# Packing sample tokens by heads, 576 projected columns, a moved sum, and S5 powers written in part as copies

## The chip, the cores and the metric

The kernel runs on one core of a Trainium2 chip. The metric is device time in microseconds (us), the median of several runs. The engines are PE (TensorE, matrix products), DVE (VectorE), ACT (ScalarE), POOL (GpSimd) and SP (SyncE, which here only issues DMAs). Each executes its own list of instructions in order, and semaphores join them.

## What is computed

Two layers of a decoder trunk for 512 prompt tokens and 8 x 8 sample tokens, 576 in all, of width 1024. Layer 0 mixes tokens with S5, a complex diagonal state space; layer 1 with causal pooling. Each mixer is followed by a layer norm and by PEER, a mixture of 16384 single-row experts:

```python
q = (x @ w_q).reshape(T, 8, 2, 128)                # 8 heads, 2 halves
s = einsum('thid,hind->thin', q, keys)              # 128 keys per half
top_s, top_i = top_k(s, 16)
cand = top_s[:, :, 0, :, None] + top_s[:, :, 1, None, :]
best_s, best_j = top_k(cand.reshape(T, 8, 256), 16)
idx  = ...                                          # key a * 128 + key b
gate = softmax(best_s)
out  = sum over h, k of  gate * gelu(x . u[idx]) * v[idx]
```

In S5 each of 64 groups has 64 complex states; u = x @ w_in is turned into inputs of the states, these run through a recurrence in time, and y is read out with the matrices C times powers of the transition.

## The kernel before

**Tokens.** The kernel carries 640 columns (NX): 384 (ND) of tiles 0 to 2, then 128 of tile 3, and 128 of tile 4 in which the 64 sample tokens stand twice. NT is 576, the tokens without the second copy. Tiles 0 to 2 go through all experts densely, tiles 3 and 4 through gathered rows.

**S5** (`s5()`). `params()` makes the powers `PW` 0 to 8. For each of eight blocks m of features, `uproj` multiplies on PE and `udone` writes u to DRAM (`du`); after m=3 and m=7 it is read back as `U8` in 16 DMAs in all, rearranged by time step. From m=4 on, `back(q)` (DVE, two `BL` tiles per call, four in rotation) multiplies b by powers 7 to 0, and `turn(q)` transposes the tiles on PE. `taps(q)` (DVE) writes c times the powers 0 to 8 into `CL`. `inputs` (PE, ACT) needs U8 and the turned tiles, `toeplitz` the taps; then the recurrence `steps` runs on DVE.

**The score loop** (`peer()`, c = 0 to 15, one half of a head each). In each iteration PE projects (`projected`: 8 blocks x 3 split products, each over two column ranges 0 to ND and ND to NX), ACT and POOL prepare the next weight (`W.ahead`: for w_q the low half `wl`, L79, is subtracted on POOL), PE multiplies the previous q with its keys (`scores`, five tiles), and DVE takes the 16 largest of each tile (`tops`, L1347 to L1355) of the one before that. Ahead of the loop POOL adds xH and xL into `xT` (L1049), in the place of tiles 0 to 2 of x, which go to DRAM first.

**The routing** (`routing`, `stage2`) is a generator that is pulled beside this: up to PA=6 steps per iteration, and an iteration stops at a step STEP. Its first two units (g = 0, 1) take four heads' halves each of all five tiles, so n8 = 10 rows of heads; a later unit takes tiles 3 and 4 with the remaining four heads, n8 = 8, the next two tiles 0 to 2. Behind the loop a second loop with hand-set credits multiplies x with experts (44 blocks per layer), gathers rows and pulls the rest of the routing. Of tile 4, rows 0 to 63 then use the entries of heads 0 to 3, rows 64 to 127 those of heads 4 to 7, so that each copy of the samples does half of them; the halves are added at the end.

**Order around it.** `norms` ends the mixer: tile by tile, layer norm on DVE, transposes on PE; the products of groups 0 and 1 over columns 0 to ND are put in early (`early`), their remainders come first in the loop. L799 is a DVE operation on one column in that norm. `finish` does the same at the end of layer 0, and the pooling mixer too calls `projected`.

Of the kernel before, what the change touches and what calls it, by code (L numbers as in the profile page):

```python
# [19 lines left out]
KD = 8  # L20
SEQ = 512
NB = 8
TS = 64
NT = SEQ + TS
NC = 72
ND = 384
NX = 640
# [12 lines left out]
BT, GB, HC, PW = 1, 32, 2.0, (1,)  # L40
GE, S3, S4 = 0.98, 100, 4
VL = (43, 44, 45)
ORDER = [a for a in range(128) if (a + 1) * NPO // 128 > a * NPO // 128]
ORDER += [a for a in range(128) if a not in ORDER]
OFF = [0, 16, 24, 29, 33, 36, 38, 40] + list(range(42, 50))
# [81 lines left out]
class K:  # L127
# [142 lines left out]
    def s5(self):  # L270
# [55 lines left out]
        def powered(jobs, a, b):  # L326

            def args(e, w):
                n, k = e.stop - e.start, len(range(9)[w])
                sh = [128, n, k, 16]  # L330
                pw = [PW[:, w, r, e].rearrange("p s e -> p e s")[:, :, :, None].to_broadcast(sh) for r in range(2)]
                return pw, [t[:, e, None, :].to_broadcast(sh) for t in (a, b)]
            todo = [(o, t) + args(e, w) for o, t, e, w in jobs]
            for o, t, pw, ab in todo:
                V.tensor_tensor(o, pw[0], ab[0], op=OP.mult)
            for o, t, pw, ab in todo:
                V.tensor_tensor(t, pw[1], ab[1], op=OP.mult)
            for o, t, pw, ab in todo:
                V.tensor_tensor(o, o, t, op=OP.subtract)

        def params():
# [14 lines left out]
                next(ex, None)  # L356
            for _ in ex:
                pass
            V.memset(PW[:, 0, 0, :], 1.0)
            V.memset(PW[:, 0, 1, :], 0.0)  # L360
            V.tensor_tensor(PW[:, 1, 0, :], mag, cs, op=OP.mult)
            V.tensor_tensor(PW[:, 1, 1, :], mag, sn, op=OP.mult)
            tmp = p2.tile([128, 4, 8, 16], F32, name="BL", bufs=4).rearrange("p a b c -> p a (b c)")[:, :, :64]
            for b in (1, 2, 4):
                sh = [128, b, 64]
                cmul(V, PW[:, b + 1:2 * b + 1, 0, :], PW[:, b + 1:2 * b + 1, 1, :],
# [3 lines left out]
            im = slice(64, 128)  # L370
            A.activation(b2[im], b2[im], AF.Copy, scale=-1.0)
            A.activation(c1[im], c1[im], AF.Copy, scale=-1.0)

            for h in range(2):
                rows, e = slice(64 * h, 64 * h + 64), slice(32 * h, 32 * h + 32)
# [18 lines left out]

            for h in range(2):
                e = slice(32 * h, 32 * h + 32)
                BL = p2.tile([128, 4, 8, 16], F32, name="BL", bufs=4)
                t = BL.rearrange("p e s j -> p (e s) j")
                V.tensor_tensor(bb[:, e], bc(fr[:, e]), b1[:, e], op=OP.mult)
                V.tensor_tensor(t, bc(fi[:, e]), b2[:, e], op=OP.mult)  # L400
                V.tensor_tensor(b1[:, e], bc(fi[:, e]), b1[:, e], op=OP.mult)
                V.tensor_tensor(b2[:, e], bc(fr[:, e]), b2[:, e], op=OP.mult)
                V.tensor_tensor(bb[:, e], bb[:, e], t, op=OP.subtract)
                V.tensor_tensor(b2[:, e], b2[:, e], b1[:, e], op=OP.add)

        def back(q):

            BL, tb = ([p.tile([128, 4, n, 16], F32, name=k, bufs=m)[:, :, :8] for _ in range(2)] for p, k, n, m in ((p2, "BL", 8, 4), (pc, "tb", 9, 2)))
            e = [slice(8 * q + 4 * i, 8 * q + 4 * i + 4) for i in range(2)]
            powered([(BL[i], tb[i], e[i], slice(7, None, -1)) for i in range(2)], bb, b2)  # L410
            return BL

        def turn(q, BL):
# [7 lines left out]
        def taps(q):  # L421

            for e0 in (8 * q, 32 + 8 * q):
                es = [slice(e0 + i, e0 + i + 4) for i in (0, 4)]
                powered([(CL[:, e], pc.tile([128, 4, 9, 16], F32, name="tb", bufs=2), e, slice(0, 9)) for e in es], c1, c2)


        params()
# [9 lines left out]
        def udone(m, o):  # L438
            uT = p2.tile([128, NT], F32, name="uT", bufs=2)
            for q in range(2):  # L440
                A.activation(uT[:, 288 * q:288 * q + 288], o[q][:, :288], AF.Copy)
            A.dma_start(du[128 * m:128 * m + 128, :], uT)
            if m % 4 == 3:
                g = slice(8 * (m - 3), 8 * m + 8)
                for s in range(8):
                    (G if m > 3 and s % 2 else S).dma_start(U8[16 * s:16 * s + 16, g, :], duv[s][:, g, :])

        first = self.W.next_raws(2)
        o = [[self.ps(), self.ps()] for _ in range(2)]
# [361 lines left out]
    def projected(self):  # L811

        if self.pre:
            w, o, a, b = self.pre.pop(0)
            c, d = (b, NX) if a == 0 else (0, a)
            outs = [(self.ps()[:, :d - c], slice(c, d))]
            self.proj(outs, w, self.xH, self.xL)
            outs.insert(0 if a == 0 else 1, (o[:, :b - a], slice(a, b)))
        else:
            outs = [(self.ps()[:, :b - a], slice(a, b)) for a, b in ((0, ND), (ND, NX))]  # L820
            self.proj(outs, self.W.next(), self.xH, self.xL)
        return outs

    def finish(self, res, ln, p, then, transposed):
# [37 lines left out]
                    for _ in tr[4]:  # L862
                        pass
        if transposed:
            self.early(ND, NX)
            for tt in range(3):
                for _ in tr[tt]:
                    pass
# [163 lines left out]
    def peer(self, layer):  # L1032
# [13 lines left out]

        S.dma_start(XD, self.x012)
        xT = self.per.tile([128, KD, ND], F32, name="x012")
        G.tensor_tensor(xT, self.xH.main.bitcast(F32), self.xL.main.bitcast(F32), op=OP.add)  # L1049
        pr = self.pool(rk, "pr")  # L1050

        it = pr.tile([128, 128], I32, name="it")
# [1 line left out]
        self.iota2 = p2.tile([128, 128, 2], F16, name="iota2")  # L1054
        A.activation(self.iota2, it[:, :, None].to_broadcast([128, 128, 2]), AF.Copy)

        tops_ = [[pr.tile([128, 2, 5, 4, 16] if q < 2 else [128, 5, 8, 16], dt, name=f"{n}{q}") for q in (0, 2)]
                 for n, dt in (("tv", F32), ("ti", U32))]
        tv, ti = (lambda tt, c, t=t: t[0][:, c // 4, tt, c % 4] if c < 8 else t[1][:, tt, c - 8] for t in tops_)
        LG = ExitStack()  # L1060
# [15 lines left out]
        keys = {}  # L1076
# [6 lines left out]
        kload(0)  # L1083
        kload(1)

        def scores(c, q):
            o = [self.psB(), self.psB()]
            sc = pq.tile([128, 5, 128], F32, name="sc", bufs=3)
            for tt in range(5):
                d = o[tt // 4][:, 128 * (tt % 4):128 * (tt % 4) + 128]  # L1090
                self.mm(d, q[:, 128 * tt:128 * tt + 128], keys[c // 4][:, c % 4, :], True, True)
            A.activation(sc[:, :4].rearrange("p a b -> p (a b)"), o[0], AF.Copy)
            A.activation(sc[:, 4], o[1][:, :128], AF.Copy)
            return sc

        def tops(c, sc):
            self.top16([(sc[:, tt], tv(tt, c), ti(tt, c)) for tt in range(5)])

        prev = prev2 = None
        for c in range(16):  # L1100
            outs = self.projected()
            self.W.ahead()
            if layer == 0:
                next(self.pt, None)
            if prev:
                s_ = (c - 1, scores(c - 1, prev))
                if c % 4 == 0 and c < 12:
                    kload(c // 4 + 1)
            q = pq.tile([128, NX], F32, name="q", bufs=2)
            for o, cols in outs:  # L1110
                A.activation(q[:, cols], o, AF.Copy)
            if prev2:
                tops(*prev2)
                self.scored = c - 2
                for _ in range(PA):
                    if self.half or next(bg) == STEP:
                        break
            prev2 = s_ if prev else None
            prev = q
# [237 lines left out]
    def routing(self, tops, p, pr, p2, rk, gidx, ggate, GD, kept, begin, ending):  # L1357
# [7 lines left out]
        for g in range(2):  # L1365
            while self.scored < 4 * g + 3:
                yield STEP
            yield from self.stage2(tv[0][:, g], ti[0][:, g], p2, [t[:, :, 32 * g:32 * g + 32] for t in out])
        self.half = 1
        yield 0.0  # L1370
        unit = lambda ts: self.stage2(tv[1][:, ts], ti[1][:, ts], p2, [t[:, ts, 64:] for t in out])
        i1, i2, gate = out
        yield from unit(slice(3, 5))
        for u in range(2):
            f = p2.tile([128, 128], F32, name="idf")
            V.scalar_tensor_tensor(f, i1[:, 3 + u], 128.0, i2[:, 3 + u], op0=OP.mult, op1=OP.add)
            if u == 0:
                V.tensor_copy(gidx[:, :128], f)
                V.tensor_copy(ggate[:, :128], gate[:, 3])
            else:  # L1380
                for q in range(2):
                    rows = slice(64 * q, 64 * q + 64)
                    V.tensor_copy(gidx[rows, 128:], f[rows, rows])
                    V.tensor_copy(ggate[rows, 128:], gate[rows, 4, rows])
        self.gready = True
        yield 1.6

# [68 lines left out]
    def stage2(self, tv, ti, p, out):  # L1456
# [3 lines left out]
        V, A = nc.vector, nc.scalar  # L1460
        nt, nh = tv.shape[1], tv.shape[2] // 2
        n8 = nt * nh
        T = lambda n, w, dt=F32: p.tile([128, 10, w], dt, name=n)[:, :n8]
        v = tv.rearrange("p t (h s) k -> p (t h) s k", s=2)
        ids = p.tile([128, 10, 2, 16], F16, name="ids")[:, :n8]
# [24 lines left out]
        rep, hot, prod = (p.tile([128, 10, 16, 16], F16, name=k)[:, :n8] for k in ("rep", "hot", "prod"))  # L1490
# [143 lines left out]
```

## Time and profile before

| | us |
|---|---|
| median of 3 runs (3198.44 to 3201.87) | 3200.0 |
| the profiled execution | 3198.16 |
| its span, first to last instruction | 3195.9 |
| PE busy | 2993.5 (94%) |
| DVE busy | 2713.2 (85%) |
| POOL busy | 1270.6 (40%) |
| ACT busy | 1150.6 (36%) |
| mean DMA rate | 270 GB/s |

Busy shares are means over stages with different limits: S5 takes the first 240 us, the score loop of layer 0 lies between 307 and 472 us, the credit loop behind it up to 748, the long stream of expert layer 0 up to 1640; layer 1 repeats the latter parts behind its pooling mixer, from 1667 on. Which engine ends a stage is read from the rows below: busy time by stretch, the chain of waits (the work that ended last, each step with its start and length), and timelines by engine, where square brackets give idle time before an instruction and what ended it.

### The profile page before, as it was taken

The page shows a single profiled execution, that of the slowest core. Times are in us where ns is not written, and L with a number is a line of the kernel's source. Part 1 is how long each engine was busy: PE and PEld are TensorE (multiplying, and loading weights), DVE is VectorE, ACT ScalarE, POOL GpSimd, SP SyncE. Part 2 cuts the span into 40 slices and gives each one's busy share as a digit, 9 for nine tenths or more (in the row PEclk, how much of TensorE's full clock was granted, in tenths as well). Part 3 has the DMA queues.
Part 4 walks back from the last instruction along what each step waited for, and adds up shares of the span by engine and source line. Part 5 has one row for each costly group of instructions (what it writes and reads, how often), then busy time and mean ns, then how long its engine had stood idle before and what let it go on. Part 6 is the DMA issues. An engine that isn't in the chain of part 4 may idle for free.

```text
span 3195.9 us, 45180 instructions
## 1 busy us (share of the span) xinstructions
PE 2993.5 (94%) x16188; PEld 2549.7 (80%) x16188; DVE 2713.2 (85%) x5872; ACT 1150.6 (36%) x1712; POOL 1270.6 (40%) x944
## 2 busy tenths in 40 slices
PE   9589989998999999999978997989899999999996
PEld 7488965666888888888878896556688888888886
DVE  8956998998888888888986689899888888888888
ACT  2451323454333333333324132245433333333332
POOL 2321214443455555555410131444344545554541
PEclk9899989999999999999999999999999999999998
DMA  5461428899999999999943121889899999999995
GB/s 164 75 204 64 182 68 297 324 370 319 324 348 332 338 342 340 336 339 347 346 167 97 66 73 55 284 312 385 304 332 330 338 337 342 340 332 351 352 335 200
DMA packets 330416, 862.42 MB, mean 270 GB/s; under 512 B 54152, under 2 KB 143272, under 8 KB 327479
## 3 DMA queue, kind: packets, MB, share of 16 engines
q1 hardware_dynamic: 202574, 433.80, 39.2%
q0 software_dynamic: 113216, 405.95, 35.1%
q10 hardware_dynamic: 14400, 19.78, 1.7%
q8 instruction: 127, 2.08, 0.3%
q14 instruction: 99, 0.80, 0.1%
HBM read 791.76 MB, written 71.96 MB: 270 GB/s over the span
## 4 chain that ended last, share of the span: by engine, by line
PE 73%; DVE 18%; DMA 5%; issue 2%; ACT 1%; POOL 1%; SPq 1%; DVEq 0%; POOLq 0%; ACTq 0%
PE pa L133 42%; PE pb L133 30%; DMA grow<-in_peer_u,gidx 1%; DVE prod L1502 1%; DVE ti L1355 1%; DVE sc L1351 1%; DVE ti L1349 1%; DVE grow L1541 1%; DMA x<-SD 1%; DVE tv L1347 1%; DVE tv L1353 1%; DVE rs L799 1%; POOL grow L1536 1%; DVE prod L1520 0%; DVE st L783 0%
## 5 line engine op out<-in xcount | busy, mean ns | idle before, releaser
L1536 POOL DMA_INDIRECT grow<-in_peer_u,gidx x384 | 608.4, 1584 | 533.2 <-DVE acc L1549 309.5
L1536 POOL DMA_INDIRECT grow<-in_peer_v,gidx x384 | 499.8, 1302 | 711.0 <-DVE grow L1541 576.8
L138 DVE TENSOR_TENSOR vl<-vr,vh 128x1024 fp32r<-128x1024 f32 x256 | 314.3, 1228 | 250.6 <-ACT vh L137 250.2
L133 PE MATMUL pa<-vh,wwh 128*128 128x512 f32 x1536 | 478.6, 393 | 25.6 <-ACT wwh L1233 25.4
L1549 DVE SCALAR_TENSOR_TENSOR acc<-grow,gact,acc 128x1024 f32<-128x1024 f32 x380 | 486.9, 1281 | 3.4 <-DMA grow<-in_peer_v,gidx 2.4
L1541 DVE SCALAR_TENSOR_TENSOR grow<-grow,x 128x1024 f32<-128x1024 f32 x384 | 466.3, 1220 | 23.4 <-DMA grow<-in_peer_u,gidx 23.3
L133 PE MATMUL pa<-vh,wwl 128*128 128x512 f32 x1536 | 477.3, 392 | 0.0
L133 PE MATMUL pa<-vl,wwh 128*128 128x512 f32 x1536 | 476.5, 392 | 0.0
L137 ACT ACTIVATE vh<-vr 128x1024 fp32r<-128x1024 f32 x256 | 271.8, 1062 | 509.9 <-PE pa L133 480.8
L133 PE MATMUL pb<-xH,wl 128*128 128x384 f32 x1344 | 455.1, 339 | 0.0
L133 PE MATMUL pb<-xH,wh 128*128 128x384 f32 x1344 | 455.0, 339 | 0.0
L133 PE MATMUL pb<-xL,wh 128*128 128x384 f32 x1344 | 454.5, 338 | 0.0
L133 PEld LDWEIGHTS pa<-vh,wwh 128*128 128x128 f32 x1536 | 287.1, 189 | 76.8 <-ACT wwh L1233 28.9
L133 PEld LDWEIGHTS pa<-vl,wwh 128*128 128x128 f32 x1536 | 289.4, 188 | 63.4
L133 PEld LDWEIGHTS pa<-vh,wwl 128*128 128x128 f32 x1536 | 288.6, 188 | 63.4 <-DVE wwl L1235 1.4
L133 PEld LDWEIGHTS pb<-xL,wh 128*128 128x128 f32 x1344 | 253.2, 188 | 7.4
L133 PEld LDWEIGHTS pb<-xH,wh 128*128 128x128 f32 x1344 | 252.4, 188 | 6.5
L133 PEld LDWEIGHTS pb<-xH,wl 128*128 128x128 f32 x1344 | 252.4, 188 | 0.0
L79 POOL TENSOR_TENSOR wl<-wr,wh 128x1024 fp32r<-128x1024 f32 x35 | 88.9, 2541 | 408.2 <-ACT wh L69 314.3
L79 DVE TENSOR_TENSOR wl<-wr,wh 128x1024 fp32r<-128x1024 f32 x185 | 225.5, 1219 | 23.7 <-ACT wh L69 23.6
L133 PE MATMUL pb<-x,wr 128*128 128x384 f32 x704 | 240.5, 496 | 0.1
L69 ACT ACTIVATE wh<-wr 128x1024 fp32r<-128x1024 f32 x220 | 230.9, 1050 | 11.3 <-PE pa L133 11.3
(341 smaller groups left out, 4853.5 us busy)
## 6 DMA issues: line engine op xcount, KB each, us to landing
wr<-in_U SPq DMA_DIRECT2D x256, 512.0 KB
vr<-in_peer_v SPq DMA_DIRECT2D x256, 512.0 KB
GD<-stg SPq DMA_DIRECT2D x16, 2048.0 KB
x<-GD SPq DMA_DIRECT2D x64, 512.0 KB
SD<-g ACTq DMA_DIRECT2D x88, 192.0 KB
x<-SD SPq DMA_DIRECT2D x88, 192.0 KB
wr<-in_w_q SPq DMA_DIRECT2D x32, 512.0 KB
grow<-in_peer_u,gidx POOLq DMA_INDIRECT x384, 7.4
```

Of the source, the lines that this page charges most:

```text
L69: self.k.nc.scalar.activation(h[:, :nk], self.raw[self.nh], AF.Copy)
L79: e.tensor_tensor(l[:, :nk], self.raw.pop(self.ns), h[:, :nk].bitcast(F32), op=OP.subtract)
L133: self.nc.tensor.matmul(out, lhsT, rhs, start=start, stop=stop)
L137: self.nc.scalar.activation(h, src, AF.Copy)
L138: self.nc.vector.tensor_tensor(l, src, h.bitcast(F32), op=OP.subtract)
L799: yield V.scalar_tensor_tensor(t, y, ve, y, op0=OP.mult, op1=OP.mult)
L1347: V.max(v[:, 0:8], s)
L1349: V.max_index(i[:, 0:8], v[:, 0:8], s)
L1351: V.match_replace(s, v[:, 0:8], s, -3.0e38)
L1536: nc.gpsimd.indirect_dma_start(out=t, out_offset=None, in_=table, in_offset=bass.IndirectOffsetOnAxis(ap=gidx[:, 128 * u + j:128 * u + j + ...
L1541: V.scalar_tensor_tensor(t, t, 1.0, self.X(3 + u), op0=OP.mult, op1=OP.mult, accum_out=act[:, 128 * u + j:128 * u + j + 1])
L1549: V.scalar_tensor_tensor(acc[:, u], t, w, acc[:, u], op0=OP.mult, op1=OP.add)
```

## The change

- S5: the zeroth power is no longer stored (two DVE memsets go). Where it was a factor, ACT copies: `c1` into `CL[:, :, 0]`, and `bb` into the last part of each BL tile. The products in `back` and `taps` have 7 and 8 powers instead of 8 and 9. BL has six tiles in rotation. u is read back after m = 3, 5, 6 and 7 (32, 16, 8 and 8 groups), eight DMAs each, always half on SP and half on POOL.
- Projections stop at column 576.
- scores: the sample tokens are projected once. For c%4 of 0 and 1 their scores go to rows 0 to 63 of a tile, for 2 and 3 to rows 64 to 127 of the same tile; `tops` handles four tiles, and with c%4 of 2 and 3 the packed one as a fifth. Rows 0 to 63 so take even heads, rows 64 to 127 odd ones, and the packed tile goes wholly into the later unit; units g = 0, 1 have 8 rows of heads.
- xT is added in three parts, in iterations 1 to 3 behind `W.ahead`.

```diff
-            V.memset(PW[:, 0, 0, :], 1.0)
-            V.memset(PW[:, 0, 1, :], 0.0)
...
+            A.activation(CL[:, :, 0], c1, AF.Copy)
...
         def back(q):
-            BL, tb = ([p.tile([128, 4, n, 16], F32, name=k, bufs=m)[:, :, :8] for _ in range(2)] for p, k, n, m in ((p2, "BL", 8, 4), (pc, "tb", 9, 2)))
+            BL, tb = ([p.tile([128, 4, 8, 16], F32, name=k, bufs=m) for _ in range(2)] for p, k, m in ((p2, "BL", 6), (pc, "tb", 2)))
             e = [slice(8 * q + 4 * i, 8 * q + 4 * i + 4) for i in range(2)]
-            powered([(BL[i], tb[i], e[i], slice(7, None, -1)) for i in range(2)], bb, b2)
+            for i in range(2):
+                A.activation(BL[i][:, :, 7], bb[:, e[i]], AF.Copy)
+            powered([(BL[i][:, :, :7], tb[i][:, :, :7], e[i], slice(7, 0, -1)) for i in range(2)], bb, b2)
             return BL
...
-                powered([(CL[:, e], pc.tile([128, 4, 9, 16], F32, name="tb", bufs=2), e, slice(0, 9)) for e in es], c1, c2)
+                powered([(CL[:, e, 1:], pc.tile([128, 4, 8, 16], F32, name="tb", bufs=2), e, slice(1, 9)) for e in es], c1, c2)
...
+UL = {3: 0, 5: 4, 6: 6, 7: 7}
...
-            if m % 4 == 3:
-                g = slice(8 * (m - 3), 8 * m + 8)
+            if m in UL:
+                g = slice(8 * UL[m], 8 * m + 8)
                 for s in range(8):
-                    (G if m > 3 and s % 2 else S).dma_start(U8[16 * s:16 * s + 16, g, :], duv[s][:, g, :])
+                    (G if s % 2 else S).dma_start(U8[16 * s:16 * s + 16, g, :], duv[s][:, g, :])
...
-            outs = [(self.ps()[:, :b - a], slice(a, b)) for a, b in ((0, ND), (ND, NX))]
+            outs = [(self.ps()[:, :b - a], slice(a, b)) for a, b in ((0, ND), (ND, NT))]
...
-        G.tensor_tensor(xT, self.xH.main.bitcast(F32), self.xL.main.bitcast(F32), op=OP.add)
...
         def scores(c, q):
             o = [self.psB(), self.psB()]
-            sc = pq.tile([128, 5, 128], F32, name="sc", bufs=3)
-            for tt in range(5):
-                d = o[tt // 4][:, 128 * (tt % 4):128 * (tt % 4) + 128]
-                self.mm(d, q[:, 128 * tt:128 * tt + 128], keys[c // 4][:, c % 4, :], True, True)
-            A.activation(sc[:, :4].rearrange("p a b -> p (a b)"), o[0], AF.Copy)
-            A.activation(sc[:, 4], o[1][:, :128], AF.Copy)
-            return sc
+            sc = pq.tile([128, 4, 128], F32, name="sc", bufs=3)
+            k, r = keys[c // 4][:, c % 4, :], slice(c % 4 // 2 * 64, c % 4 // 2 * 64 + 64)
+            for tt in range(4):
+                self.mm(o[0][:, 128 * tt:128 * tt + 128], q[:, 128 * tt:128 * tt + 128], k, True, True)
+            self.mm(o[1][r, :128], q[:, SEQ:], k, True, True)
+            A.activation(sc.rearrange("p a b -> p (a b)"), o[0], AF.Copy)
+            if c % 4 < 2:
+                sc4[c % 4] = pq.tile([128, 128], F32, name="sc4", bufs=4)
+            A.activation(sc4[c % 2][r], o[1][r, :128], AF.Copy)
+            return sc, sc4[c % 2]
 
         def tops(c, sc):
-            self.top16([(sc[:, tt], tv(tt, c), ti(tt, c)) for tt in range(5)])
+            sets = [(sc[0][:, tt], tv(tt, c), ti(tt, c)) for tt in range(4)]
+            if c % 4 > 1:
+                sets.append((sc[1],) + tuple(t[1][:, 4, 2 * (c // 4) + c % 2] for t in tops_))
+            self.top16(sets)
...
             self.W.ahead()
+            if 0 < c < 4:
+                ks = slice(3 * c - 3, min(3 * c, KD))
+                G.tensor_tensor(xT[:, ks], *(t.main[:, ks].bitcast(F32) for t in (self.xH, self.xL)), op=OP.add)
...
-            yield from self.stage2(tv[0][:, g], ti[0][:, g], p2, [t[:, :, 32 * g:32 * g + 32] for t in out])
+            yield from self.stage2(tv[0][:, g], ti[0][:, g], p2, [t[:, :4, 32 * g:32 * g + 32] for t in out])
```

Not shown: the tiles of `stage2` and of the maxima shrink to match, the second column range in `finish` and `projected` ends at NT, and the indices of tile 4 are written from columns 64 to 127 alone.

## Rows read from the trace of the kernel before

**Rows 1.** Busy time by stretch: engines, PE clock, DMA share, GB/s

```profile
core 0: us, PE busy (x) PEld busy (x) DVE busy (x) ACT busy (x) POOL busy (x), PEclk, DMA share, GB/s
1000.00:1300.00 300.00, 300.00 (x1479) 269.25 (x1478) 254.37 (x402) 108.28 (x146) 154.48 (x107) 1.00 0.94 336
339.00:455.00 116.00, 97.25 (x669) 95.69 (x668) 114.01 (x627) 38.43 (x66) 29.46 (x11) 0.93 0.31 114
472.50:582.00 109.50, 97.91 (x309) 57.79 (x308) 96.96 (x340) 28.32 (x42) 47.19 (x37) 0.94 0.82 296
```

**Rows 2.** Chain of waits (start us, length us, what), norm and loop, layers 0, 1

```profile
288.24 6.83 DVE rs L799
...
306.88 7.16 PE pa L133 x47
...
315.15 6.89 PE pa L133 x48
...
1829.82 8.35 PE pa L133 x47
```

**Rows 3.** Chain of waits in the score loop of layer 0 and behind it

```profile
353.16 0.22 DVE bs L1347 x2
...
354.78 0.24 DVE jf L1483
...
362.83 3.47 DVE prod L1510
...
413.92 1.40 DVE hot L1508
415.35 1.50 DVE prod L1510
...
419.26 0.24 DVE b L1513
...
466.71 0.95 DVE tv L1347 x5
...
472.58 0.29 DVE ids L1466
...
482.24 1.23 DVE hot L1508
...
486.80 0.22 DVE b L1513
...
495.42 0.30 DVE idf L1376
```

**Rows 4.** Timeline of POOL (start, length, instruction, idle before), norm and loop

```profile
288.22 6.82 POOL L1049 TENSOR_TENSOR x<-xH,xL 128x3072 f32<-128x3072 f32 x1 [1.62 <-DVE rs L800]
...
317.47 2.42 POOL L79 TENSOR_TENSOR wl<-wr,wh 128x1024 fp32r<-128x1024 f32 x1 [2.34 <-issue]
```

**Rows 5.** Timeline of DVE in S5, 65 to 106 us

```profile
65.20 1.29 DVE L335 TENSOR_TENSOR BL<-PW,bb 128x512 f32<-128x512 f32 x2 [1.96 <-PE pb L417]
...
69.95 1.29 DVE L335 TENSOR_TENSOR BL<-PW,bb 128x512 f32<-128x512 f32 x2 [1.05 <-PE pb L417]
...
73.57 1.42 DVE L335 TENSOR_TENSOR CL<-PW,c 128x576 f32<-128x576 f32 x2
...
106.05 0.71 DVE L552 TENSOR_TENSOR w<-AP,HS 128x512 f32<-128x512 f32 x1
```

**Rows 6.** Timeline of PE in S5

```profile
97.69 6.04 PE L133 MATMUL pa<-U,BT 128*64 128x72 f32 x128 [5.77 <-issue]
```

**Rows 7.** Timeline of PE at the end of the norm, layer 0

```profile
304.84 1.06 PE L908 MATMUL pb<-ident,x 128*128 128x128 f32 x8 [2.22 <-DVE x L801]
```

**Rows 8.** Instructions of L1349 (count: ns min/median/max, first to last start us)

```profile
L1349 DVE FIND_INDEX8 ti<-tv,sc x160: 272/284/329, 316.6 to 1992.5; 128x8 uint32<-128x128 f32 x160
```

**Rows 9.** Chain of waits in the pooling mixer

```profile
1667.58 50.27 PE pa L133 x336
1717.86 1.23 DVE wl L79
```

**Rows 10.** DMA issues, 30 to 110 us: count, size, median us to landing

```profile
T<-KT POOLq DMA_DIRECT2D x2, 32.0 KB, 3.8
```

More of the change, by code (lines that the diff above doesn't have):

```diff
@@ L358, in params @@
                 pass
-            V.memset(PW[:, 0, 0, :], 1.0)
-            V.memset(PW[:, 0, 1, :], 0.0)
             V.tensor_tensor(PW[:, 1, 0, :], mag, cs, op=OP.mult)
             V.tensor_tensor(PW[:, 1, 1, :], mag, sn, op=OP.mult)
-            tmp = p2.tile([128, 4, 8, 16], F32, name="BL", bufs=4).rearrange("p a b c -> p a (b c)")[:, :, :64]
+            tmp = p2.tile([128, 4, 8, 16], F32, name="BL", bufs=6).rearrange("p a b c -> p a (b c)")[:, :, :64]
             for b in (1, 2, 4):
@@ L396, in params @@
                 e = slice(32 * h, 32 * h + 32)
-                BL = p2.tile([128, 4, 8, 16], F32, name="BL", bufs=4)
+                BL = p2.tile([128, 4, 8, 16], F32, name="BL", bufs=6)
                 t = BL.rearrange("p e s j -> p (e s) j")
@@ L814, in projected @@
             w, o, a, b = self.pre.pop(0)
-            c, d = (b, NX) if a == 0 else (0, a)
+            c, d = (b, NT) if a == 0 else (0, a)
             outs = [(self.ps()[:, :d - c], slice(c, d))]
@@ L864, in finish @@
         if transposed:
-            self.early(ND, NX)
+            self.early(ND, NT)
             for tt in range(3):
@@ L1055, in peer @@
         A.activation(self.iota2, it[:, :, None].to_broadcast([128, 128, 2]), AF.Copy)
-        tops_ = [[pr.tile([128, 2, 5, 4, 16] if q < 2 else [128, 5, 8, 16], dt, name=f"{n}{q}") for q in (0, 2)]
+        tops_ = [[pr.tile([128, 2, 4, 4, 16] if q < 2 else [128, 5, 8, 16], dt, name=f"{n}{q}") for q in (0, 2)]
                  for n, dt in (("tv", F32), ("ti", U32))]
@@ L1084, in peer @@
         kload(1)
+        sc4 = {}
         def scores(c, q):
             o = [self.psB(), self.psB()]
-            sc = pq.tile([128, 5, 128], F32, name="sc", bufs=3)
-            for tt in range(5):
-                d = o[tt // 4][:, 128 * (tt % 4):128 * (tt % 4) + 128]
-                self.mm(d, q[:, 128 * tt:128 * tt + 128], keys[c // 4][:, c % 4, :], True, True)
-            A.activation(sc[:, :4].rearrange("p a b -> p (a b)"), o[0], AF.Copy)
-            A.activation(sc[:, 4], o[1][:, :128], AF.Copy)
-            return sc
+            sc = pq.tile([128, 4, 128], F32, name="sc", bufs=3)
[8 more added lines that the diff above has]
+            return sc, sc4[c % 2]
         def tops(c, sc):
-            self.top16([(sc[:, tt], tv(tt, c), ti(tt, c)) for tt in range(5)])
+            sets = [(sc[0][:, tt], tv(tt, c), ti(tt, c)) for tt in range(4)]
+            if c % 4 > 1:
+                sets.append((sc[1],) + tuple(t[1][:, 4, 2 * (c // 4) + c % 2] for t in tops_))
+            self.top16(sets)
         prev = prev2 = None
@@ L1108, in peer @@
                     kload(c // 4 + 1)
-            q = pq.tile([128, NX], F32, name="q", bufs=2)
+            q = pq.tile([128, NT], F32, name="q", bufs=2)
             for o, cols in outs:
@@ L1373, in routing @@
         yield from unit(slice(3, 5))
-        for u in range(2):
+        for u, c in ((0, slice(0, 128)), (1, slice(64, 128))):
             f = p2.tile([128, 128], F32, name="idf")
[L1376 to L1384, printed above, removed]
+            V.scalar_tensor_tensor(f[:, c], i1[:, 3 + u, c], 128.0, i2[:, 3 + u, c], op0=OP.mult, op1=OP.add)
+            o = slice(64 * u + c.start, 64 * u + c.stop)
+            V.tensor_copy(gidx[:, o], f[:, c])
+            V.tensor_copy(ggate[:, o], gate[:, 3 + u, c])
         self.gready = True
@@ L1462, in stage2 @@
         n8 = nt * nh
-        T = lambda n, w, dt=F32: p.tile([128, 10, w], dt, name=n)[:, :n8]
+        T = lambda n, w, dt=F32: p.tile([128, 8, w], dt, name=n)[:, :n8]
         v = tv.rearrange("p t (h s) k -> p (t h) s k", s=2)
-        ids = p.tile([128, 10, 2, 16], F16, name="ids")[:, :n8]
+        ids = p.tile([128, 8, 2, 16], F16, name="ids")[:, :n8]
         V.tensor_copy(ids, ti.rearrange("p t (h s) k -> p (t h) s k", s=2))
@@ L1489, in stage2 @@
         sh = [128, n8, 16, 16]
-        rep, hot, prod = (p.tile([128, 10, 16, 16], F16, name=k)[:, :n8] for k in ("rep", "hot", "prod"))
+        rep, hot, prod = (p.tile([128, 8, 16, 16], F16, name=k)[:, :n8] for k in ("rep", "hot", "prod"))
         yield STEP
```

## The prediction

> **What bounds the kernel now.** The page first: PE is busy for most of the span, so the first question is where a saving elsewhere can show at all. The stages answer differently. In the long streams of the expert layers (1000 to 1300 us, for one) PE is busy 300.0 of 300 us at clock 1.00 [rows 1], and the change leaves them alone. In the score loop of layer 0, from 339 to 455 us, DVE is busy 114.0 of 116 us and PE 97.3 [rows 1]: there DVE sets the end. The chain of waits says the same and shows a seam. From 306.9 to 339 us it runs through PE, one product of 48 matmuls in 6.89 us per group of heads [rows 2]; after that it stays on DVE (maxima, then stage2 of the routing) until the routing's next unit begins at 472.58 [rows 3]. Layer 1 repeats it. Then the timeline by engine, for what stands ahead of each seam. In the layer norm before the loop a DVE instruction on one column takes 6.83 us [rows 2], and the only long thing beside it is POOL's sum xH+xL, 6.82 us from 288.22 [rows 4]. In S5 DVE multiplies powers without a gap from 69.95, writes taps from 73.57 and reaches the recurrence at 106.05 [rows 5]; PE stood idle 5.77 us until 97.69 for u to come back [rows 6].
>
> **The change part by part.** Times are of the profiled execution (3198.16 us, span 3195.9).
>
> *The sum xH+xL* leaves the head of peer() for iterations 1 to 3, behind W.ahead. It frees the stalled column operation, 6.6 us per layer beyond its usual 0.2. Not all arrives: PE's order puts the early product of group 1 ahead of the transposes of tile 4, and PE idles only 2.22 us between the two [rows 7]. I count 2.2 per layer (bounds 0 and 2.2; the other 4.4 go to waits of the norm for PE). The idle has a second price: the 47 matmuls behind it take 7.16 us in layer 0 and 8.35 in layer 1 [rows 2]; at 6.89 us for 24 pairs of 640 columns, 0.45 ns per column, their 256 columns would need 5.4. So 1.7 and 2.9 us come back if PE no longer pauses (0 if it still does). What the moved work meets: POOL's queue holds the low halves of w_q, 2.42 us each [rows 4]. A third of the sum is 2.3 to 2.6 us by 6.82, so POOL has 5 us of work in an iteration in which PE has at least 6.2 (6.89-0.69), and the next low half is not ready to start before PE has left its buffer. Nothing late. DVE beside it runs maxima, and of 160 index searches of one form, many beside such subtractions, the slowest took 0.33 us [rows 8]: price nothing.
>
> The Trainium skill (SBUF — State Buffer, Who interferes with whom) says that a DVE instruction with two SBUF inputs and a GpSimd instruction that reads SBUF shut each other out for a whole instruction. The stalled column operation agrees. Read strictly it would speak against the new place too, if the search counts as having two inputs; [rows 8] says that it does not wait. By the rule the time would be that of rival 4 below, by the row it is the forecast's.
>
> *576 columns.* 64 fewer of 640 are 64 x 0.45 = 29 ns per pair of matmuls, 0.69 us per group of 24 pairs. It counts where PE is the bound: the two remainders of groups 0 and 1 (48 x 64 columns, 1.4 us per layer), groups 2 to 4 (2.1 per layer), and the pooling projections, where the chain stays on PE for 336 matmuls and 50.27 us, then goes to DVE's low half of a weight [rows 9]. Eight times 0.69 is 5.5 there; DVE's windows end that stage, so I take 4.0 (2.5 to 5.5). In groups 5 to 15 DVE decides and the columns are worth nothing. Should the weight load and not the columns pace a matmul, all of this is 0; the fifth score matmul, with half its weights, I count at nothing.
>
> *The maxima.* Groups with c%4 of 0 or 1 handle four tiles, the others four and the packed fifth. One call on five tiles takes 472.58-466.71 = 5.87 us [rows 3], 1.17 per tile. In the DVE-bound stretch lie calls 3 to 15; 4, 5, 8, 9, 12 and 13 lose a tile: 6 x 1.17 = 7.0 us per layer. The others lie under PE.
>
> *Stage2 on 8 heads instead of 10* (units g=0, 1 of each layer). The third round of maxima disappears: 354.78-353.16 = 1.6 us. From the comparison to b it is 419.26-413.92 = 5.34 us with 10 and 486.80-482.24 = 4.56 with 8, 17% more; the whole of that part with 8 takes 495.42-482.24 = 13.2 us, so 2.25 us are saved. 3.9 per unit, 7.8 per layer. The order of work is the same: one yield fewer in the first part, but each iteration still stops at the same STEP, so both units end in iteration 12, and the later credits see no changed unit. A bound on this: the multiplication at 362.83 took 3.47 us where the same at 415.35 took 1.50 [rows 3]; POOL's subtraction lay beside it. Such meetings will fall elsewhere; one adds or gives 2 us, a layer has about three: 5 us either way.
>
> So the DVE stretch loses 14.8 us per layer. PE needs 6.2 us and the score matmuls for a group; DVE has needed (472.58-339)/13 = 10.3 per call and will need 9.1, so PE stays ahead. The loop after it (472.5 to 582) has PE busy 97.9 of 109.5 [rows 1]. PE starts it after its last scores, which wait for DVE; with 18 tiles instead of 20 left at that point it gets 2.3 us less head start, and the idle 11.6 absorb them. The stretch shifts as a whole.
>
> *S5.* With six tiles instead of four, back(q) waits for turn(q-3): the last one starts where the one before it did, at 65.20, not 69.95 [rows 5]. The zeroth powers become ACT copies (ACT is idle most of this time), so each product has 7 of 8 and 8 of 9 parts. taps then begin near 73.57-4.75-0.4 = 68.4; their 106.05-73.57 = 32.5 us become 28.9 (8/9 of all but the KT additions): DVE reaches the recurrence at 97.4, 8.7 us earlier. The other input, u: the last read now carries 8 groups, not 32. PE's wait ended at 97.69 with the large pieces; a small POOL transfer (32 KB) lands in 3.8 us [rows 10], which puts the last piece near 91. PE then needs 6.04 us [rows 6] and ACT half a microsecond: 97.6. Both meet near 98, 7.7 us earlier. If u lands no sooner, the start is 104.3 and the gain 1.7. What is moved: the first 8 reads are now half on POOL, and SP waits at m=5 and 6 for u to be written; behind it in SP's queue stand weights of the gate, which are used only behind the whole recurrence. Price nothing; an unhidden wait there would show as PE idle at m=6 or 7.
>
> *Sum.* S5 7.7; norms 2.2+2.2, clock 1.7+2.9, remainders 1.4+1.4; groups 2 to 4: 2.1+2.1; DVE stretch 14.8+14.8; pooling 4.0. Together 57.3. 3198.16-57.3 = 3140.9; the median of the runs is 1.8 above the profiled one, which gives 3143.
>
> **The rivals.** (1) *u comes back no sooner* because many short rows and not their number per transfer hold it: -6.0, 3149 us. For it: the reads waited long; against: the small transfer of [rows 10]. (2) *Weight loads pace a matmul of 192 columns*: columns give nothing, 57.3-2.8-4.2-4.0, 3154 us. Against it: 640 columns run at 0.45 ns each, with two loads in them. (3) *More meetings of fp16 products with POOL*: DVE's faster pace puts every low half (some 7 per layer in that stretch) beside such a product: four more per layer at 2 us, 3159 us. (4) *The moved sum blocks the maxima* as the old one blocked the column operation: if none of it falls into DVE's waits for PE in iterations 1 to 3, 6.8 us per layer, 3157 us. (5) *Slower*: with shorter pauses ahead, the two streams (some 860 us each) no longer get full clock. They run at 1.00 now [rows 1]; a mean of 0.967 would cost 57 us, so below that the kernel is slower, 3215 us at 0.96. Nothing in the rows points to it: the stream is PE-bound before and after. (6) *The change doesn't do what it says*: what is saved ahead of the loops is waited for in them, since transfers there take 0.82 of the engines [rows 1]; then only S5 and pooling count and layers give nothing: 3188 us, and without S5 no change. Against it: no transfer of that stretch starts before the indices are ready.
>
> **How the numbers follow.** Forecast 0.60; (1) 0.10, (2) 0.08, (3) 0.10, (4) 0.03, (5) 0.04, (6) 0.05, of which 0.02 at no change. The likeliest is 3143 us. Bounds: all small ends together (S5 1.7, no clock, meetings against) give 35, all large ends 71; 3128 to 3165 holds the forecast and (1) to (4). A measurement of this kernel can tell about 0.2%, 6 us. Faster 0.94, same 0.02, slower 0.04.
>
> **What would show it.** After: no column operation over 2.0 us in the norms; the transposes of tile 4 without 2 us of idle before them; in the PE-bound groups 6.2 us for 48 matmuls; four or five maxima per call; hot, prod on 2048 elements only; ids of the third unit some 22 us earlier after the loop's start is aligned to S5; the recurrence at 98 us. Wrong would be: a PE wait on POOL's low half in groups 2 to 5, PE idle in m=6 and 7, or streams below clock 0.98.

## The result, and the profile after

The changed kernel takes 3156.66 us (median; 3153.2 to 3159.24), the kernel before beside it 3199.22: a ratio of 0.9867, 95% interval 0.985 to 0.9884. The profiled execution took 3159.24 us with a span of 3157.5, against 3198.16 and 3195.9. It is 1.3% faster, and inside the range; the forecast of 3143 was 14 us too low. Of the 57.3 us of the sum the medians show 42.6, and the two profiles, the changed kernel's being the slowest of its four executions, 38.4 by their spans. Where the other 19 went is the question of this part.

The milestones come first. Chain of waits of the kernel before (start us, length us, what): the product behind S5's recurrence, the first gather of layer 0, the end of its stream, the first out projection behind the pooling mixer, the first gather of layer 1.

```profile
149.05 4.50 PE pa L133 x62
...
496.25 1.03 POOL grow L1536
...
1636.25 3.73 DMA grow<-acc
...
1764.61 15.43 PE pa L133 x65
...
2020.04 0.99 POOL grow L1536
```

The same of the changed kernel:

```profile
140.06 12.62 PE pa L135 x190
...
469.26 1.02 POOL grow L1545
...
1612.33 3.71 DMA grow<-acc
...
1737.91 15.42 PE pa L135 x65
...
1975.35 0.99 POOL grow L1545
```

Each difference says how much has been gained up to there: 9.0, 27.0, 23.9, 26.7, 44.7 us, and 38.4 at the end. So something is **given back** behind the first gather of each layer, 3.1 and 6.3 us. The start of the gate (182.80, now 172.64), of the remainders and of the score loop lie in between (the last two in [rows 2] and below), and the terms stand like this:

| term | forecast | measured, layer 0 + layer 1 |
|---|---|---|
| S5, to the start of the gate | 7.7 | 10.2 |
| norms | 2.2 + 2.2 | 2.5 + 2.4 |
| clock and remainders, with the ten score matmuls behind them | 3.1 + 4.3 | 1.5 + 2.7 |
| score loop to the first gather | 16.9 + 16.9 | 12.8 + 12.9 |
| pooling | 4.0 | 2.8 |
| behind the first gather | 0 | -3.1 - 6.3 |
| sum | 57.3 | 38.4 |

Chain of waits of the changed kernel from the end of the norm on, and the remainders of layer 1; it answers [rows 2]:

```profile
294.24 5.50 PE pa L135 x47
299.73 1.27 PE pb L135 x10
301.00 7.07 PE pa L135 x48
...
309.35 7.07 PE pa L135 x48
...
1800.77 5.50 PE pa L135 x47
```

The 6.83 us of the norm's column operation and PE's pause are gone. But the products of a group take 7.07 us where 6.2 was forecast and 6.89 stood before [rows 2], and ten score matmuls stand with 1.27, before with 1.11:

```profile
322.05 1.11 PE pb L133 x10
```

A group's period is 8.35 us, not shorter than the 8.0 of before but longer. PE is the bound until 342 us, for five groups of 48 (301.00 to 341.44) where it was three in the kernel before.

The DVE-bound part; it answers [rows 3]:

```profile
424.53 0.76 DVE tv L1361 x4
...
429.20 0.76 DVE tv L1361 x4
```

A call on four tiles takes 429.20-424.53 = 4.67 us, 1.20 less than one on five [rows 3]: as forecast. S5 answers [rows 5]: taps from 67.69 (chain of waits; forecast 68.4), the recurrence from 96.91 (timeline of DVE; forecast 98, before 106.05), and PE's products with BT without the idle of [rows 6] (group of instructions: busy, mean ns, and idle before):

```profile
67.69 1.21 DVE CL L337 x2
```

```profile
96.91 0.68 DVE L555 TENSOR_TENSOR w<-AP,HS 128x512 f32<-128x512 f32 x1
```

```profile
L135 PE MATMUL pa<-U,BT 128*64 128x72 f32 x256 | 8.6, 227 | 0.0
```

In the pooling mixer the chain leaves PE after 287 matmuls of 6.89 us per 48, where [rows 9] gave 7.18:

```profile
1643.64 41.22 PE pa L135 x287
```

### The profile page after: what moved, and what is told of

Same layout as the page of the kernel before. It is cut to its first block, busy times and chain, and to the rows that moved or that the text cites. A ratio compares the mean times of both kernels' runs of the same rounds, so it can differ in the third digit from the quotient of the medians.

```text
span 3157.5 us, 45057 instructions
## 1 busy us (share of the span) xinstructions
PE 2992.2 (95%) x16188; PEld 2542.6 (81%) x16188; DVE 2659.2 (84%) x5674; ACT 1151.0 (36%) x1729; POOL 1273.7 (40%) x960
## 4 chain that ended last, share of the span: by engine, by line
PE 75%; DVE 16%; DMA 5%; issue 2%; ACT 2%; SPq 0%; POOL 0%; DVEq 0%; ACTq 0%; POOLq 0%
PE pa L135 45%; PE pb L135 30%; DMA grow<-in_peer_u,gidx 2%; DVE prod L1511 1%; DVE grow L1550 1%; DMA x<-SD 1%; DVE ti L1369 1%; DVE sc L1365 1%; DVE ti L1363 1%; DVE tv L1367 1%; DVE tv L1361 1%; DVE prod L1533 0%; DMA wr<-in_U 0%; DVE hot L1517 0%; DVE prod L1519 0%
```

## The experiments

Theory A: a matmul of fewer than 256 columns is hardly cheaper, because something that does not shrink with its columns paces it, its weights' load most likely; the new split 384+192 so wastes what the 64 columns save. Its rival B: the group is slow for what runs beside it. For the loss behind the first gather, theory L: PE starts the expert products later relative to the first gather (its lead is shorter), and more of their weights are fetched beside the gathers. Its rivals: chance, or something else.

**Cutting at 320.**

```diff
+CUT = 320
...
-            outs = [(self.ps()[:, :b - a], slice(a, b)) for a, b in ((0, ND), (ND, NT))]
+            outs = [(self.ps()[:, :b - a], slice(a, b)) for a, b in ((0, self.xH.off), (self.xH.off, NT))]
...
+                self.xH.off = self.xL.off = CUT
...
+            dst = {2: [(0, c, 0, 128), (1, 0, 64, 128)], 3: [(1, 64, 0, 128)], 4: [(1, 192, 0, 64)]}[tt]
```

The last 64 columns of tile 2 so go to the tail as well.

> The changed kernel with its 576 columns cut at 320 instead of 384 (in front of and in the score loops of both layers; the last 64 columns of tile 2 are copied to the tail as well), so that every pair of matmuls has 320 and 256 columns. Theory A (a matmul under 256 columns is paced by something that does not shrink with its columns, so 384+192 costs 0.295 us per pair while the 288+288 pairs of the gate cost 0.267): 48 matmuls in 6.4 to 6.5 us instead of 7.07, an early product of 320 columns in 3.6 instead of 4.23, some 4 us per layer ahead of the first set DVE bounds, and a longer lead of PE ahead of the gathers; 3144 to 3150 us. Theory B (the group is slow because of what runs beside it, not because of its columns): 48 matmuls stay at 7.07 and the time at 3154 to 3160 us.

Measured: 3146.97 us (3145.43 to 3150.52), ratio 0.9842 (0.9828 to 0.9855). Chain of waits of its loop:

```profile
295.65 5.84 PE pa L136 x47
...
310.59 6.46 PE pa L136 x48
```

The same 576 columns, cut elsewhere, take 6.46 us instead of 7.07, and the time falls by 9.7 us. A holds: a pair's time does not go by the sum of its columns; B, by which it would have stayed at 7.07, is out. The 47 remainders alone bear it out from the other side: with 256 columns 5.84/47 = 124 ns each, with 192 (after) 5.50/47 = 117. A quarter fewer columns is worth 6%. The timelines show how. First weight loads (PEld) of the changed kernel's remainders; then matmuls of a pair in the kernel before, of a group at the granted clock 1.00; then the same of the changed kernel, at the same clock:

```profile
296.01 0.19 PEld L135 LDWEIGHTS pa<-xHt,wl 128*128 128x128 f32 x1
296.13 0.19 PEld L135 LDWEIGHTS pa<-xHt,wh 128*128 128x128 f32 x1
```

```profile
318.04 0.28 PE L133 MATMUL pa<-xLt,wh 128*128 128x256 f32 x1
318.16 0.33 PE L133 MATMUL pa<-xH,wl 128*128 128x384 f32 x1
318.33 0.28 PE L133 MATMUL pa<-xHt,wl 128*128 128x256 f32 x1
```

```profile
311.00 0.25 PE L135 MATMUL pa<-xHt,wl 128*128 128x192 f32 x1
311.09 0.36 PE L135 MATMUL pa<-xH,wh 128*128 128x384 f32 x1
311.29 0.25 PE L135 MATMUL pa<-xHt,wh 128*128 128x192 f32 x1
```

Alone, the matmuls of 192 columns follow their weights' loads, which start some 0.11 us apart. In a pair, the matmul behind 192 columns starts after 0.09 us, behind 256 after 0.12; but then the one behind the 384 starts after 0.20 instead of 0.17. What the narrow matmul saves, the wide one gives back, and a pair lasts 0.29 us either way. That it is the load and no other fixed price is read from these rows and not tested: no run changed the loads of the products. The Trainium skill (TensorE: Matmul & The Clock Gate, LDWEIGHTS (loading the stationary operand)) puts a load of weights at their columns divided by 1.2 ns, which is an estimate of 107 ns for 128; these spacings, and score matmuls of 128 columns at 1.11/10 = 111 ns, lie at or just above it.

**640 columns again**, and then the fifth score matmul with all 128 weights.

```diff
-            outs = [(self.ps()[:, :b - a], slice(a, b)) for a, b in ((0, ND), (ND, NT))]
+            outs = [(self.ps()[:, :b - a], slice(a, b)) for a, b in ((0, ND), (ND, NX))]
```

(The early remainders and the pooling mixer get 640 columns too; q keeps them, and the scores still read 576.)

> The changed kernel with 640 columns projected again (both layers and the pooling mixer); the scores still read 576. Theory A: 48 matmuls take 6.89 us again instead of 7.07, the 47 matmuls ahead of the loop 5.4 to 5.5 us as with 192 columns, the time is 0 to 4 us shorter than the changed kernel's. If the columns had paid as forecast (0.69 us per group), it would be 8 to 11 us longer.

```diff
-            self.mm(o[1][r, :128], q[:, SEQ:NT], k, True, True)
+            self.mm(o[1][:, :128], q[:, SEQ:], k, True, True)
```

> As the 640 columns, and the fifth score matmul with 128 weights again instead of 64 (its second half of rows is not read). If the half of the weights at an offset is what makes ten score matmuls take 1.27 instead of 1.11 us, they take 1.11 again and the time falls by another 1 to 2 us; if 64 weights cost no more than 128, they stay at 1.27.

Measured: 3159.27 us (ratio 0.9873, 0.9858 to 0.9888) and 3156.36 us (0.986, 0.9845 to 0.9875). With 640 columns the time is 2.6 us over the changed kernel's and not 0 to 4 under it, inside the intervals: the 64 columns are worth nothing that a time can tell. Two groups in a row of the first, then of the second (chains):

```profile
301.88 7.09 PE pa L135 x48
...
310.22 7.38 PE pa L135 x48
317.61 1.25 PE pb L135 x10
```

```profile
302.60 7.20 PE pa L135 x48
...
310.91 6.89 PE pa L135 x48
317.81 1.11 PE pb L135 x10
```

Two things at once. Every second group takes 0.3 us longer in both, which the score loop of the kernel before did not show (its pooling mixer, with 7.18, stood near the slower pace); my 6.89 came for half of them, and why they alternate is open. And two groups last 16.98 us with the half fifth score matmul, 16.32 with the whole one: **0.33 us per group for 64 weights less** (the samples' columns of q are the weights of that matmul). It is not the place of the half: the groups with it in rows 0 to 63 and in 64 to 127 cost the same. So a group of the changed kernel, 8.35 us against 8.01 before, is longer by this alone. Its products are those of the quicker pace, 6.89 us, and some 0.17 of waiting at their start. Against the mean of the 640 columns' two paces, 8.49 us a group, the 64 columns save 0.14, a fifth of the 0.69. Of the 0.33, 0.16 lie in the ten score matmuls (1.27 for 1.11); the timeline shows the place of the rest. First PE, then its weight loads, of the changed kernel:

```profile
317.62 0.44 PE L135 MATMUL pa<-xH,wh 128*128 128x384 f32 x1
```

```profile
317.62 0.19 PEld L135 LDWEIGHTS pa<-xH,wh 128*128 128x128 f32 x1 [0.17 <-issue]
```

and with the whole fifth matmul:

```profile
318.65 0.19 PEld L135 LDWEIGHTS pa<-xH,wh 128*128 128x128 f32 x1
```

Behind the matmul of 64 weights the next load of 128 begins only when its own matmul does (317.62 both), after an idle of 0.17 us; with equal shapes no idle is seen before the load.

**The sum back at the head.**

```diff
+        G.tensor_tensor(xT, self.xH.main.bitcast(F32), self.xL.main.bitcast(F32), op=OP.add)
...
-            if 0 < c < 4:
-                ks = slice(3 * c - 3, min(3 * c, KD))
-                G.tensor_tensor(xT[:, ks], ...)
```

> The changed kernel with POOL's sum of xH and xL back at the head of the layer. Theory: the column operation of the norm takes 6.8 us again, PE pauses 2.2 us before the last transposes and the 47 matmuls behind it take 7.2 us in layer 0 and 8.3 in layer 1: 2.2+1.7 and 2.2+2.7, together 8.8 us longer than the changed kernel. Rival: the sum only stands beside a stall that has another cause; then the stall is not back and the time stays. Second rival: what is lost ahead of the loop is made up by a longer lead later, then the norm shows the stall and the time moves by under 4 us.

Measured: 3165.41 us (ratio 0.9898, 0.9883 to 0.9913), 8.8 us more than the changed kernel. Norm of layer 0 (chain):

```profile
279.54 6.83 DVE rs L802
...
298.18 8.46 PE pa L135 x47
```

The stall is back, and the 47 matmuls take 8.46 us against 5.50. That this is the clock shows in the busy time by stretch (columns as in [rows 1]; PEclk is the third from the end), here and in the changed kernel:

```profile
298.18:306.64 8.46, 8.46 (x49) 8.46 (x50) 0.54 (x1) 1.67 (x4) 2.22 (x1) 0.63 0.01 3
```

```profile
294.24:299.73 5.49, 5.49 (x49) 5.49 (x50) 0.54 (x1) 1.67 (x4) 1.56 (x1) 1.00 0.02 6
```

The mean granted clock is 0.63 behind the norm with its pause, between the two levels of 1.2 and 2.4 GHz (0.5 and 1.00), and 1.00 without the pause; in the kernel before it was 0.80 over the 7.16 us of layer 0 and 0.66 over the 8.35 of layer 1. Both first-order prices of the forecast, the pause and the clock, are real and reach the end. In its new place the sum stalls nothing: of the index searches of the changed kernel's first loop (count: ns min/median/max), which answer [rows 8], the slowest took 0.29 us.

```profile
L1363 DVE FIND_INDEX8 ti<-tv,sc x72: 276/284/289, 302.2 to 441.7; 128x8 uint32<-128x128 f32 x72
```

**Both cures together**, with three and with four buffers of scores; four buffers on the changed kernel alone; and the changed kernel once more. The samples' columns stand between tiles 1 and 2 in q, so that a window of 128 columns with the samples in either half exists.

```diff
+            for tt, a in enumerate((0, 128, 320, 448)):
+                self.mm(o[0][:, 128 * tt:128 * tt + 128], q[:, a:a + 128], k, True, True)
+            a = 256 - r.start
+            self.mm(o[1][:, :128], q[:, a:a + 128], k, True, True)
```

> The 320/256 cut of the earlier run, and the fifth score matmul with 128 weights: the samples' columns stand between tile 1 and tile 2 in q, and each window of 128 columns takes 64 neighbours along, whose rows of the result are not read. Theory (the matmul of 64 weights between matmuls of 128 costs about 0.3 us per group, 1.35 us for ten score matmuls from the first start to the next product's start, against 1.04 with 128 weights): the period of a PE-bound group falls from 7.70 to 7.40 us, 2 us per layer of which the lead into the gathers takes a part; 3142 to 3146 us. Rival (the 0.3 us belong to the 192 columns or to the row offset): period 7.70, 3145 to 3150 us.

```diff
-            sc = pq.tile([128, 4, 128], F32, name="sc", bufs=3)
+            sc = pq.tile([128, 4, 128], F32, name="sc", bufs=4)
```

> The same with four buffers of scores instead of three, so that PE may run one group further ahead of DVE's maxima. Theory of the lead (what was lost after the indices comes from PE starting the expert products 34 us ahead of the first gather instead of 40): the lead rises to 40 us or more, the stretch from the first gather to the combining matmuls falls from 85 to about 82 us in both layers, 3135 to 3142 us. Rival (that stretch is set by DVE and the gathers alone): lead up, stretch stays at 85 to 88, the time is that of three buffers.

> The changed kernel with four buffers of scores instead of three, nothing else. In the DVE-bound stretch of layer 0 PE waited 8.3 us. Theory of the lead: the waits go, the lead rises from 34 to about 40 us, the stretch from the first gather to the combining matmuls falls from 86 and 91 us to 83 to 86, 3147 to 3153 us. Rival: the lead rises and nothing follows, 3153 to 3159 us.

> The changed kernel once more, as the measure for the runs beside it: 3153 to 3160 us; lead 34 us in both layers. If the stretch from the first gather to the combining matmuls, 86 and 91 us in its first profile, comes out 5 us apart between the layers again, something differs between the layers; if not, it varies from one execution to the next by some 5 us.

Measured: 3144.71 us (ratio 0.9837, 0.9824 to 0.9851), 3148.49 (0.9852, 0.9833 to 0.987), 3156.33 (0.9871, 0.9854 to 0.9888) and 3156.65 (0.9878, 0.9861 to 0.9894). The first is the lowest median of all, though not apart from the 320 cut alone. Its groups:

```profile
301.43 6.25 PE pa L136 x48
307.67 1.11 PE pb L136 x10
```

A period of 7.36 us: with both cures the loop has the 6.2 us that the forecast wrote down. And with them the score loop, from there to the first gather (465.8), lasts 164.4 us, against 181.1 before and 168.3 after: 16.7 us less, where 16.9 were forecast. The DVE terms were right; PE's groups ate their start.

The fourth buffer changed nothing: PE's lead, from its first expert product to the first gather, was 37.6 us with both cures (37.5 with three buffers) and 34.0 and 34.7 in the two layers without them (34.4 and 34.0), where 40 was expected. PE's one long wait in the loop of layer 0, 6.1 us, has another cause. ACT's timeline in the changed kernel:

```profile
387.42 1.91 ACT L1501 ACTIVATE rep<-jf 128x2048 f16<-128x2048 f16 x1 [10.33 <-DVE jf L1492]
...
389.44 1.04 ACT L71 ACTIVATE wh<-wr 128x1024 fp32r<-128x1024 f32 x1
```

ACT stands 10.33 us before a copy for the routing that waits for DVE, and PE's next weight is behind it in ACT's queue.

**PE held back** for the test of theory L.

```diff
         s_ = (15, scores(15, prev))
+        o = self.ps()
+        for i in range(40):
+            self.mm(o[:, :ND], self.xH.main[:, i % KD, :128], self.xH.main[:, i % KD, :], i == 0, i == 39)
```

> The changed kernel with 40 matmuls of 384 columns more behind the last scores of each layer (a product that nobody reads, some 7 us of PE), so that the lead of the expert products ahead of the first gather falls from 34 to 27 us. Theory of the lead (weights of U that PE still has to fetch beside the gathers slow the gathers, 0.6 us for each us of lead lost): the stretch from the first gather to the combining matmuls grows from 87.5 us (mean of twelve stretches at a lead of 34) to some 91 to 92, 3163 to 3168 us. Rival (DVE's 74 us and waits for rows that change from one execution to the next, whatever the lead): 84 to 90 us as before, 3153 to 3160 us.

Measured: 3169.14 us (ratio 0.9906, 0.9889 to 0.9923), 12.5 us more, and not by the way that either theory had. The lead fell only to 32.5 us and not to 27, because the first gather came later too: from the loop's start 173.0 us instead of 168.3. Its chain:

```profile
432.27 26.86 PE pa L135 x112
459.15 0.50 ACT g L1170
...
460.04 1.92 ACT rep L1504
```

It is the same queue, the other way round: the routing's copy `rep` stands behind the activation of an expert product, and that waits for PE. How near this is can be read from ACT's idle ahead of `rep`, before (first) and after:

```profile
480.29 1.91 ACT L1492 ACTIVATE rep<-jf 128x2048 f16<-128x2048 f16 x1 [8.21 <-DVE jf L1483]
```

```profile
453.30 1.91 ACT L1501 ACTIVATE rep<-jf 128x2048 f16<-128x2048 f16 x1 [1.88 <-DVE jf L1492]
```

8.21 us of room have become 1.88. Some 7 us of holding less 1.9 leaves 5.1 per layer, near the 4.7 seen in layer 0 (4.9 in layer 1).

**The parts of S5**: the old two reads of u; four tiles instead of six.

```diff
-UL = {3: 0, 5: 4, 6: 6, 7: 7}
+UL = {3: 0, 7: 4}
...
-                    (G if s % 2 else S).dma_start(U8[16 * s:16 * s + 16, g, :], duv[s][:, g, :])
+                    (G if m > 3 and s % 2 else S).dma_start(U8[16 * s:16 * s + 16, g, :], duv[s][:, g, :])
```

> The changed kernel with u read back in two pieces of 32 groups as before, the rest of S5 as changed. Theory of the forecast: PE waits again for u ahead of its products with BT (5.8 us of idle in the kernel before, now more, because DVE comes earlier), S5 gives 1.7 to 3 us of its 9 to 10, 3162 to 3165 us. Rival: the taps alone set the end and u's pieces give nothing, 3153 to 3159 us.

```diff
-            BL = p2.tile([128, 4, 8, 16], F32, name="BL", bufs=6)
+            BL = p2.tile([128, 4, 8, 16], F32, name="BL", bufs=4)
```

> The changed kernel with four tiles for the powers instead of six (the copies of the zeroth powers and the four pieces stay). Theory of the forecast: DVE's taps begin 4.4 us later again, near 72, and the recurrence with them, since both inputs met at the same time; 3160 to 3162 us. Rival: u comes later than the taps anyway, then less than 1.5 us.

Measured: 3164.33 us (ratio 0.9889, 0.9872 to 0.9905) and 3162.43 us (0.9884, 0.9867 to 0.99), 7.7 and 5.8 us more. The product behind the recurrence starts at 146.41 and 145.53 instead of 140.06 (149.05 before). With the old reads PE again waits 5.9 us ahead of its products with BT:

```profile
L135 PE MATMUL pa<-U,BT 128*64 128x72 f32 x256 | 10.2, 251 | 5.9 <-issue 5.9
```

DVE then reaches the recurrence's start at 97.40 and waits 6.04 us for the inputs, until 103.44, near the 104.3 that the forecast gave for this case. With four tiles the taps begin at 73.18, and the recurrence at 102.49. Each undoing alone loses some 6 of 9 us: two inputs that meet, and neither part gives much without the other. The old reads put back both the size of the pieces and their queue, so which of these counts is not shown; nor were the copies of the zeroth powers taken out alone.

**The kernel before once more.**

> The kernel before once more, for a second profile of its stretch from the first gather to the combining matmuls (84.4 and 86.4 us in the first). If what was lost there belongs to the change, it shows 84 to 87 us in both layers against a mean of 87.5 after; if it varies by itself, values up to 90 us.

Measured: 3196.98 us (ratio 0.9996, 0.9985 to 1.0006). From the first gather to the combining matmuls its layers took 84.15 and 86.45 us, with the first profile 84.2 and 86.4 in the mean; in the eight profiles with a lead of 34 to 35 us (the changed kernel twice, and with four buffers, 640 columns twice, the sum at the head, either part of S5 undone) 83.7 to 87.6 and 85.7 to 90.7, in the mean 86.3 and 88.5. So some 2 us per layer seem to belong to the change; single executions lie up to 2.8 us from the mean, and of the kernel before there are only two profiles. DVE works 74 us in each such stretch; what differs is its waiting for rows (before, then after, layer 1: sum, times, longest):

```profile
DVE grow L1541 <- DMA grow<-in_peer_u,gidx: 10.9, 6, 3.8
```

```profile
DVE grow L1550 <- DMA grow<-in_peer_u,gidx: 15.6, 5, 4.9
```

Theory L is neither shown nor refuted. The means of both layers are 85.3 us at a lead of 40 (before), 87.4 at 34 to 35 and 88.7 at 32.5 (held), as it would have it; but 85.3 at 36.4 (cut at 320) and 88.2 at 37.5 (both cures), and the one run that was to decide it hardly moved the lead. The transfers fill 0.90 to 0.95 of the DMA engines' time in this stretch before and after. What makes the rows come later stays open.

## Why the prediction was right and where it failed

*S5*: right in its two parts and in that both must come; 7.7 forecast, 9.1 at the recurrence's start (96.91, forecast 98), 9.0 behind it and 10.2 at the gate; where the last 1.2 came from was not followed. The earlier end of `back` and the 8/9 of the taps came as worked out (taps from 67.69 for 29.2 us, forecast 68.4 and 28.9).

*The sum*: right. The pause was 2.2 us and the rest went to other waits, 2.5 and 2.4 measured; undoing it costs 8.8 us. The clock's return was put a little too high, 1.7 and 2.9: 256 columns at clock 1.00 take 5.84 us and not 5.4, which leaves 1.3 and 2.5.

*Columns*: **the step that failed**. "64 x 0.45 = 29 ns per pair" took a mean over a pair of 384 and 256 for a price per column. Rival 2, "weight loads pace a matmul of 192 columns", is what happened, with a forecast chance of 0.08. Two rows of the trace of before would have told. Ten score matmuls of 128 columns take 1.11 us, 111 ns each, where 0.45 ns per column would make 58: a narrow matmul had a floor. And the gate multiplies 576 columns as 288+288, 48 of them in 6.40 us (chain of the kernel before), which bounds what 576 columns can cost when neither part is narrow:

```profile
195.30 6.40 PE pa L133 x48
```

A row with the number of columns of the new tile, or the next smaller, not a slope through another one, was the nearest bound. The remainders gave 0.3 us per layer for 1.4, the groups nothing against the kernel before instead of 0.69 each, and pooling gave 2.8 instead of 4.0, going from near the slower pace of a pair to the quicker one.

*The fifth score matmul*, which "I count at nothing", costs 0.33 us per group, half of what the columns were to give, and made the groups longer than before. It had no bound from both sides in the sum, and should have had one.

*Maxima and stage2*: 14.8 us per layer, right in size (1.20 per tile, 16.7 of 16.9 once PE's groups are fast; stage2's share was not measured by itself), but 4 of them per layer fell under PE's longer groups. "PE stays ahead" held for the later groups and failed for the first.

*"The stretch shifts as a whole"* failed: 3.1 and 6.3 us were lost behind the gather in this profile, of which some 2 per layer are the mean over the other profiles too; the rest is this execution's own and that of the streams behind (the second profile of the changed kernel has a span of 3153.4). The reason that was given, PE's idle 11.6 us, looked at the wrong thing: what waits there is DVE, for rows.

The other rivals: u came back sooner (1), the moved sum blocked nothing (4), the streams kept their clock (1.00 from 1000 to 1300 us as before, 0.99 over the whole of each) (5). Of long DVE operations beside POOL's subtraction (3) each layer's chain shows three (2.49 to 3.31 us), as many as the forecast had counted and not four more. The time of rival 2 alone, 3154, is within 3 us of the measured one, and that is partly luck: S5 gave 2.5 us more than its term, and the fifth score matmul and the stretch behind the gathers, which rival 2 does not have, took some back. Of (6), savings that are waited for in the loops behind, the 3.1 and 6.3 us are a small part come true.

## What to carry to other kernels

Before columns are taken off a matmul, look for a row of the same weights with the width that it is to have: from 256 to 192 columns a matmul alone went from 124 to 117 ns here, a pair kept its 0.29 us, and cutting the same 576 at 320 instead of 384 was worth 10 us. When a bound engine is relieved, ask how much room the next one has, not only whether it is faster on average: ACT's idle ahead of one copy (8.2, then 1.9 us) was that number. A queue in which one engine serves two others ties these to each other in both directions.

## What the runs showed of the hardware

- Pairs of fp32r matmuls at clock 1.00, by group of 24: 384+256 columns 6.89 or 7.20 us, 384+192 6.89 (pooling mixer), 320+256 6.25, 288+288 6.40. Behind a matmul of 64 weights the first three take 7.09 or 7.38, 7.07, and 6.45 to 6.59.
- One matmul of 64 weights between such of 128 costs 0.33 us a group: the next load started with its own matmul, after 0.17 us of idle, and not ahead of it.
- With a pause of PE and the norm's waits ahead, the granted clock of 47 matmuls was 0.63 to 0.80; without the pause 1.00.
- The same 48 matmuls of 384+256 columns ran at two paces in one kernel, every second group 0.3 us longer; what differs between the groups was not found.
